# RWKV-7 stage of a hybrid trunk: one two-bank tile with one eviction, a block-diagonal solve, one state update for both heads, and the output products behind it

## The chip, the cores and the metric

The kernel runs on one core of a Trainium2 chip. The metric is the device time of one execution in microseconds (us). Engines are named as the profile names them: PE is the matrix engine (TensorE), PEld its weight loads, DVE the vector engine, ACT the scalar engine, POOL GpSimd, SP the engine that issues DMAs. PSUM is the memory that PE writes and DVE and ACT read; it has eight banks of 512 fp32 columns on 128 partitions.

## The reference

One layer of an encoder on `x` (1 x 4096 tokens x 1024 features): an RMS norm, one input projection whose columns feed three groups of heads, an output projection, an RMS norm and a residual. Group A is a Mamba-2 scan, group C a cross attention into 256 memory tokens. The change lies in group B, RWKV-7, with four heads of 64:

```python
def rwkv7_recurrence(r, w, k, v, a_vec, b_vec):
    """S_t = S_{t-1} (diag(w_t) + a_t^T b_t) + v_t^T k_t ; y_t = S_t r_t. Inputs (b,l,h,d) float32."""
    def step(S, inp):
        r_t, w_t, k_t, v_t, a_t, b_t = inp
        sa = jnp.einsum('bhij,bhj->bhi', S, a_t)
        S = S * w_t[:, :, None, :] + sa[..., None] * b_t[:, :, None, :] + v_t[..., None] * k_t[:, :, None, :]
        return S, jnp.einsum('bhij,bhj->bhi', S, r_t)
    ...

def rwkv7_group(u, mu, w0, w2, a0, a2, k_k, k_a, r_k, lnx_w, lnx_b):
    ...                                     # token shift, decay, k, kk, a from the projection u
    y = rwkv7_recurrence(rh, hs(decay), kh, vh, -kk, kk * ah)
    mean = jnp.mean(y, axis=-1, keepdims=True)
    var = jnp.mean(jnp.square(y - mean), axis=-1, keepdims=True)
    y = (y - mean) * lax.rsqrt(var + LNX_EPS)
    y = y * lnx_w... + lnx_b...
    bonus = jnp.sum(rh * kh * r_k, axis=-1, keepdims=True) * vh
    return ((y + bonus).reshape(b, l, W) * jax.nn.silu(g)).astype(u.dtype)
```

## The kernel before, in words

The program has three phases in one launch: `phase_a` (the Mamba-2 group, to about 750 us), `phase_b` (RWKV-7, to about 1640 us) and `phase_c` (attention and output projection). The code is written as generators; `weave` calls several of them in turn by weights, and the framework's scheduler, which has its own model of times, sets the order of every engine when the program is built. On the chip each engine then works through its row in that order and waits on semaphores where an operand isn't there.

`phase_b` goes over the 4096 tokens in 16 steps of `NT` = 256 tokens; a step has `NC_` = 4 chunks of `C` = 64 tokens, and the four heads are two pairs `p_` of two heads `h`. A pair fills the 128 partitions: head 0 lies in partitions 0 to 63 and head 1 in 64 to 127. What one step does is spread over three rounds of the loop: while step i is projected, the inverse of step i-1 is computed and the state runs through step i-2. The generators of a step:

- `stage1` projects the normalised tokens. Each weight goes through PE as three products of high and low parts (`w_hi`, `w_lo` by `hh`, `hl`; L137), 128x128 stationary and 256 columns. This is most of PE's work. It then forms r, k, v, the decay and so on.
- `gram2` makes, for each pair, four chunks and two heads, a 128x128 Gram product of `BK` by `AR` (L730). Head 0 goes to the PSUM bank `ps_yd`, head 1 to `ps_st`; DVE multiplies each bank by a mask into `AT` (L733).
- `solve2` inverts the triangular part of each 64x64 block: a recurrence on DVE for blocks of 16, then 32x16 products on PE (L785 to L815) that put larger blocks together in `TT`, two heads one above the other, 64 partitions by 64 columns each.
- `tokmaj` turns `v` and `BK` by transposes into rows of tokens (`UV`, `BKt`; L833, L846), and `stack` copies a part of `AR` under `AT` (L859).
- `stage3` is the serial part, chunk after chunk: ACT copies the state `ST` into `UV` (L871), POOL scales it to `S0` (L873), four products `AT` by `UV` give a right-hand side (L878), ACT copies that to `X` (L881), four 64x64 products `TT` by `X` solve (L885), DVE copies one head of the result to `UV` and ACT the other (L890), four products `BKt` by `UV` give the update (L895), and DVE adds it to `S0` for the next `ST` (L898). All of a chunk's products lie in one PSUM bank, `ps_yo`. After every second chunk, 16 output products of 64 columns follow: `rr` by `ST` (L912) and `AT` by `UV` (L915), into `ps_yd` for head 0 and `ps_st` for head 1.
- `stage4` normalises the outputs: DVE takes the means of both banks (L927), POOL scales them (L928), DVE centres both banks (L931); after that the banks are free. The result is scaled, gated and stored.

PSUM tiles come from one pool `ps` by tag: `tr` (2 buffers), `pj` (2), and `g`, `yo`, `yd`, `st` (one each). So `yd` and `st` serve the Gram products of step i-1 and the outputs of step i-2 by turns; the last step's Gram products go to `g` and `tr`.

Of the kernel before, what the change touches and what calls it, by code (L numbers as in the profile page):

```python
# [14 lines left out]
P = 128  # L15
# [12 lines left out]
def tile_hymba_trunk(  # L28
# [17 lines left out]

    def psum(tag, bufs):
        return ps.tile([P, 512], F32, name="ps_" + tag, tag=tag, bufs=bufs)
# [118 lines left out]
    def phase_a():  # L167
        a_l, a_r = ExitStack(), ExitStack()
# [324 lines left out]
    def phase_b(a_tail, a_l):  # L493
# [198 lines left out]
        left = lambda nm: b_l.enter_context(tc.tile_pool(name=nm, bufs=1, reuse_waits="tile"))  # L692
        bo.append(left("bo1"))
# [16 lines left out]
        nct = bi.tile([P, 16, 2 * NPC], F32, name="nct")  # L710
# [10 lines left out]

        def gram2(i, r):
            AR, BK, ec = r["AR"], r["BK"], r["ec"]
            AT = bi.tile([P, NPC, 2, P], F32, name="AT", tag="AT", bufs=2)
            for p_ in range(2):
                pas = (psum("g", 1), ps_tr()) if i == NS - 1 else (psum("yd", 1), psum("st", 1))
# [5 lines left out]
                for h, pa in enumerate(pas):  # L732
                    v.tensor_tensor(out=AT[:, p_ * NC_:(p_ + 1) * NC_, h, :], in0=pa.rearrange("p (x t) -> p x t", t=P),  # L733
                                    in1=amask.unsqueeze(1).broadcast_to([P, NC_, P]), op=ALU.mult)
                    yield
# [5 lines left out]
        def solve2(i, r):  # L741
            AT = r["AT"]
            for q in range(4):
# [31 lines left out]
            TT = bw.tile([P, NPC, 2, 32], F32, name="TT", tag="TT", bufs=2)  # L775
            Df = bi.tile([P, NPC, 32], F32, name="Df", tag="Df", bufs=2)
            Dt = bi.tile([P, NPC, 32], F32, name="Dt", tag="Dt")
# [74 lines left out]
        def stack(r):  # L852

            while "TT" not in r:
                yield
            AR, AT = r["AR"], r["AT"]
            for h in range(2):
                hs = slice(h * 64, h * 64 + 64)
                s.copy(out=AT[hs, :, h, 0:C].rearrange("p (b c) t -> p b c t", b=2), in_=AR[hs, :, :, 0, :])  # L859

        def stage3(i, r, nxt=None):
            AT, TT = r["AT"], r["TT"]
            pys = [psum("yd", 1), psum("st", 1)]
            sts = []
            for c_ in range(NC_):
# [16 lines left out]
                for p_, pc in enumerate(pcs):  # L882
                    for h in range(2):
                        hs = slice(h * 64, h * 64 + 64)
                        te.matmul(pch[hs, 128 + p_ * C:128 + p_ * C + C], lhsT=TT[hs, pc].rearrange("p a t -> p (a t)"),  # L885
                                  rhs=X[hs, p_, :], start=True, stop=True)
                yield
                for h in range(2):
                    hs = slice(h * 64, h * 64 + 64)
                    (s.copy if h else v.tensor_copy)(out=UV[hs, c_::NC_, h, :],  # L890
                                                     in_=pch[hs, 128:256].rearrange("p (b t) -> p b t", b=2))
# [402 lines left out]
```

## Time and profile before

| | |
|---|---|
| runs, us | 2230.16, 2230.88, 2237.77 (median 2230.88) |
| profiled execution | 2231.82 us, its span 2230.1 us |
| mean granted clock of PE | 0.983 of full speed |
| PE busy in 0 to 749 us (`phase_a`) | 717.96 of 749 us, DVE 594.15, ACT 395.01, POOL 274.65 |
| PE busy in 750 to 1640 us (`phase_b`) | 861.41 of 890 us, DVE 635.89, ACT 569.96, POOL 306.30 |
| PE busy in 1640 to 2230 us (`phase_c`) | 579.22 of 590.1 us, DVE 280.43, ACT 218.98, POOL 132.67 |

How to read the lines that follow: one execution was recorded by the hardware profiler. A line of the timeline gives the start of a group of like instructions in us, its length from first start to last end, the engine, the source line, the output and inputs by the program's names, the part of PE's array that the stationary operand uses, the shape, and behind x the number of records; in brackets stands how long the engine waited just before and for whom. A line of the groups gives the count, the busy time in us, the mean ns of one, and behind the bar the idle time of the engine just before them with what ended it. Lengths of matmuls overlap, since PE is pipelined; what a matmul costs PE is seen from start to start.

### The profile page before, as it was taken

Reading aid. Unit: us, or ns where it says so; the run is one execution under the profiler, and the core shown is the slowest. Engines: PE = TensorE matmul, PEld = TensorE weight load, DVE = VectorE, ACT = ScalarE, POOL = GpSimd, SP = SyncE. Lnnn points to the kernel's source line nnn. Section 1 sums busy time; section 2 is a strip of 40 time slices with the busy share of each in tenths; the row PEclk is TensorE's granted clock in tenths of the full one; section 3 lists DMA queues with packets and bytes.
Section 4 is the critical chain, followed back from the end, with each engine's and each line's share of the span. In section 5 each row is a group of like instructions: output and inputs, shape, how many; then the busy total and the mean of one; then the engine's idle time right before and its main releaser. Section 6 shows DMA issues by size and latency. Waiting matters only on the chain.

```text
span 2230.1 us, 51100 instructions
## 1 busy us (share of the span) xinstructions
PE 2159.6 (97%) x20705; PEld 1990.6 (89%) x20705; DVE 1511.5 (68%) x3442; ACT 1184.1 (53%) x2877; POOL 714.6 (32%) x1039
## 2 busy tenths in 40 slices
PE   5999999999999889999999999999899999999998
PEld 4999999999999888898899898898888888888986
DVE  5788878878888887577677777777574345454452
ACT  6555555545554565566666666677653334333341
POOL 1343434434343343343333433333112222222123
PEclk8999999999999999999999999999899999999999
DMA  6233222322233331112111112114243334334232
GB/s 204 86 135 103 96 96 93 141 91 96 96 114 132 114 99 39 44 44 76 50 49 44 44 48 78 49 59 146 91 161 132 130 112 143 127 120 137 103 123 76
DMA packets 83610, 218.86 MB, mean 98 GB/s; under 512 B 9191, under 2 KB 45486, under 8 KB 71086
## 3 DMA queue, kind: packets, MB, share of 16 engines
q1 hardware_dynamic: 82334, 215.59, 27.9%
q8 instruction: 163, 2.67, 0.5%
q14 instruction: 73, 0.60, 0.1%
q10 hardware_dynamic: 1040, 0.00, 0.0%
HBM read 152.00 MB, written 63.57 MB: 97 GB/s over the span
## 4 chain that ended last, share of the span: by engine, by line
PE 84%; DVE 6%; DMA 4%; ACT 3%; issue 1%; POOL 1%; SPq 0%; POOLq 0%; ACTq 0%; DVEq 0%
PE ps_pj L137 39%; PE ps_pj L147 8%; PE ps_yd L147 8%; PE ps_st L147 8%; DVE cc L296 2%; PE ps_yd L425 1%; PE ps_yo L878 1%; PE ps_pj L1143 1%; PE ps_yd L730 1%; PE ps_tr L126 1%; DMA w_st<-in_w_in_dram 1%; PE ps_tr L1131 1%; DMA R<-rowd 1%; PE ps_yo L885 1%; PE ps_st L417 1%
## 5 line engine op out<-in xcount | busy, mean ns | idle before, releaser
L137 PE MATMUL ps_pj<-hh,w_hi 128*128 128x256 f32 x2704 | 791.0, 293 | 6.8 <-ACT w_hi L78 4.0
L137 PE MATMUL ps_pj<-hh,w_lo 128*128 128x256 f32 x2704 | 781.1, 289 | 2.2 <-DVE w_lo L79 2.1
L137 PE MATMUL ps_pj<-hl,w_hi 128*128 128x256 f32 x2704 | 778.9, 288 | 0.0
L137 PEld LDWEIGHTS ps_pj<-hh,w_hi 128*128 128x128 f32 x2704 | 520.5, 192 | 17.9 <-ACT w_hi L78 4.6
L137 PEld LDWEIGHTS ps_pj<-hh,w_lo 128*128 128x128 f32 x2704 | 520.2, 192 | 9.7 <-DVE w_lo L79 3.5
L137 PEld LDWEIGHTS ps_pj<-hl,w_hi 128*128 128x128 f32 x2704 | 521.0, 193 | 7.1
L296 DVE SCALAR_TENSOR_TENSOR cc<-ux,cwh,cc 128x256 f32<-128x256 f32 x384 | 220.3, 616 | 16.0 <-ACT cc L293 12.2
L147 PE MATMUL ps_pj<-w_hi,hh 128*128 128x260 f32 (+1 forms) x528 | 156.6, 297 | 21.3 <-DVE dtr L270 15.8
L147 PE MATMUL ps_pj<-w_hi,hl 128*128 128x260 f32 (+1 forms) x528 | 153.0, 290 | 0.0
L147 PE MATMUL ps_pj<-w_lo,hh 128*128 128x260 f32 (+1 forms) x528 | 152.3, 289 | 0.0
L147 PEld LDWEIGHTS ps_pj<-w_hi,hh 128*128 128x128 f32 x528 | 102.5, 194 | 23.7 <-issue 16.0
L1150 DVE TENSOR_TENSOR ya<-ps_pj,ya 64x256 f32<-64x256 f32 x64 | 26.9, 421 | 121.6 <-ACT ya L1149 121.3
L1183 POOL TENSOR_TENSOR xr<-ot,xr 128x512 f32<-128x512 f32 x64 | 89.3, 1418 | 42.4 <-DVE ot L1182 42.4
L147 PEld LDWEIGHTS ps_pj<-w_lo,hh 128*128 128x128 f32 x528 | 102.5, 194 | 0.3
L147 PEld LDWEIGHTS ps_pj<-w_hi,hl 128*128 128x128 f32 x528 | 102.2, 194 | 0.0
L1177 POOL TENSOR_TENSOR sq<-sq 128x1 f32<-128x1 f32 x32 | 6.4, 201 | 292.7 <-ACT ot L1175 292.7
L147 PE MATMUL ps_yd<-wo0h,yh 128*128 128x512 f32 x248 | 98.3, 396 | 0.0
L147 PE MATMUL ps_st<-wo1l,yh 128*128 128x512 f32 x248 | 97.7, 394 | 0.4 <-DVE wo1l L1244 0.4
L147 PE MATMUL ps_st<-wo1h,yh 128*128 128x512 f32 x248 | 97.5, 393 | 0.0
L147 PE MATMUL ps_st<-wo1h,ylo 128*128 128x512 f32 x248 | 97.4, 393 | 0.0
L147 PE MATMUL ps_yd<-wo0h,ylo 128*128 128x512 f32 x248 | 97.3, 392 | 0.0
L147 PE MATMUL ps_yd<-wo0l,yh 128*128 128x512 f32 x248 | 97.2, 392 | 0.0
(474 smaller groups left out, 5102.1 us busy)
## 6 DMA issues: line engine op xcount, KB each, us to landing
hl<-hTd SPq DMA_DIRECT2D x32, 1024.0 KB
hh<-hTd SPq DMA_DIRECT2D x32, 1024.0 KB
xt<-in_x_dram SPq DMA_DIRECT2D x32, 512.0 KB
hTd<-hh SPq DMA_DIRECT2D x16, 1024.0 KB
hTd<-hl SPq DMA_DIRECT2D x16, 1024.0 KB
R<-rowd SPq DMA_DIRECT2D x32, 512.0 KB
xr<-in_x_dram SPq DMA_DIRECT2D x32, 512.0 KB
out_dram<-xr SPq DMA_DIRECT2D x32, 512.0 KB
```

What stands on the lines that cost most here:

```text
L126: te.transpose(pt[:, q * P:(q + 1) * P], src[:, k * P:(k + 1) * P], ident)
L137: te.matmul(outp, lhsT=a[:, k, :], rhs=b[:, k, :], start=(n == 0), stop=(n == 3 * KB - 1))
L147: te.matmul(outp, lhsT=a[:, k, tsl], rhs=b[:, k, 0:ncol], start=(n == 0), stop=(n == 3 * KB - 1))
L296: v.scalar_tensor_tensor(out=cc[:, b_, :], in0=ux[:, b_, j:j + NT], scalar=wj(j), in1=cc[:, b_, :], op0=ALU.mult, op1=ALU.add)
L417: te.matmul(pst[:, gr * 256:gr * 256 + 256], lhsT=q[c]["btm"][:, gr * P:(gr + 1) * P], rhs=q[c]["xde"][:, gr * 256:gr * 256 + 256], start= ...
L425: te.matmul(yd[hf * 64:hf * 64 + 64, h * 64:h * 64 + 64], lhsT=R[:, h, hf * 64:hf * 64 + 64], rhs=xdt[:, h * 64:h * 64 + 64], start=True, ...
L730: te.matmul(pa[:, c_ * P:(c_ + 1) * P], lhsT=BK[hs, p_, c_].rearrange("p a t -> p (a t)"), rhs=AR[hs, p_, c_].rearrange("p a t -> p (a t)" ...
L878: te.matmul(pch[hs, p_ * C:p_ * C + C], lhsT=AT[:, pc, h, 0:C], rhs=UV[:, pc, h, :], start=True, stop=True)
L885: te.matmul(pch[hs, 128 + p_ * C:128 + p_ * C + C], lhsT=TT[hs, pc].rearrange("p a t -> p (a t)"), rhs=X[hs, p_, :], start=True, stop=True)
L1131: te.transpose(pt[:, o:o + P], pr[:, t, m_ * P:(m_ + 1) * P], ident)
L1150: v.tensor_tensor(out=ya[hs], in0=pg[hs], in1=ya[hs], op=ALU.add)
L1183: g.tensor_tensor(out=xr[:, cs], in0=ots[n_], in1=xr[:, cs], op=ALU.add)
```

## The change

It has six parts.

1. The tags `yd` and `st` leave the pool `ps`. Each phase opens a pool of its own for them (`two_banks`); in `phase_b` that pool holds one tile `two` of two banks, [128, 2, 512], with one buffer.
2. `gram2` puts both heads in that tile, and one DVE instruction masks both banks (L751 of the changed kernel). `stage3` puts the outputs of both heads there, and `stage4` has one mean and one centring (L952, L955). The Gram products of the last step go to `g` and `tr` as before.
3. A tile `TTb` holds `TT` of both heads as a block-diagonal 128x128 matrix per chunk and pair. It is cleared once; `stack` fills the diagonal blocks with two POOL copies a step. The solve is then one 128x128 product over 64 columns per pair (L908), so two per chunk instead of four.
4. The update is one product per pair with all of `BKt` as stationary operand and both heads' `UV` as 128 columns (L917), two per chunk instead of four. Half of the result is not wanted; DVE adds the wanted parts to `S0` with two instructions on 64 partitions each (L922).
5. The output products stand under `tc.issue_after(upd.ins)`, which has them ordered right behind the last update product.
6. In `solve2` two pairs of work tiles share a buffer and `TT` has one buffer instead of two; a step waits with it until `stack` of the step before has run.

```diff
+        TTb = bw.tile([P, NPC, 2, C], F32, name="TTb")
+        g.memset(TTb, 0.0)
+        two = lambda: psx[-1].tile([P, 2, 512], F32, name="ps_two", tag="two", bufs=1)
 ...
-                pas = (psum("g", 1), ps_tr()) if i == NS - 1 else (psum("yd", 1), psum("st", 1))
+                big = None if i == NS - 1 else two()
+                pas = (psum("g", 1), ps_tr()) if big is None else (big[:, 0, :], big[:, 1, :])
 ...
-                for h, pa in enumerate(pas):
-                    v.tensor_tensor(out=AT[:, p_ * NC_:(p_ + 1) * NC_, h, :], in0=pa.rearrange("p (x t) -> p x t", t=P),
-                                    in1=amask.unsqueeze(1).broadcast_to([P, NC_, P]), op=ALU.mult)
+                    v.tensor_tensor(out=AT[:, p_ * NC_:(p_ + 1) * NC_].rearrange("p x h t -> p h x t"),
+                                    in0=big.rearrange("p h (x t) -> p h x t", t=P),
+                                    in1=amask.unsqueeze(1).unsqueeze(1).broadcast_to([P, 2, NC_, P]), op=ALU.mult)
 ...
-            TT = bw.tile([P, NPC, 2, 32], F32, name="TT", tag="TT", bufs=2)
+            while i > 0 and "stacked" not in rs_[i - 1]:
+                yield
+            TT = bw.tile([P, NPC, 2, 32], F32, name="TT", tag="TT")
 ...
+                g.tensor_copy(out=TTb[hs, :, h], in_=r["TT"][hs].rearrange("p c a t -> p c (a t)"))
                 s.copy(out=AT[hs, :, h, 0:C].rearrange("p (b c) t -> p b c t", b=2), in_=AR[hs, :, :, 0, :])
 ...
-            pys = [psum("yd", 1), psum("st", 1)]
+            py = two()
 ...
-                    for h in range(2):
-                        hs = slice(h * 64, h * 64 + 64)
-                        te.matmul(pch[hs, 128 + p_ * C:128 + p_ * C + C], lhsT=TT[hs, pc].rearrange("p a t -> p (a t)"),
-                                  rhs=X[hs, p_, :], start=True, stop=True)
+                    te.matmul(pch[:, 128 + p_ * C:128 + p_ * C + C], lhsT=TTb[:, pc].rearrange("p h t -> p (h t)"),
+                              rhs=X[:, p_, :], start=True, stop=True)
 ...
-                    for h in range(2):
-                        hs = slice(h * 64, h * 64 + 64)
-                        te.matmul(pch[hs, 256 + p_ * C:256 + p_ * C + C], lhsT=BKt[:, pc, hs], rhs=UV[:, pc, h, :],
-                                  start=True, stop=True)
+                    upd = te.matmul(pch[:, 256 + p_ * P:256 + p_ * P + P], lhsT=BKt[:, pc, :],
+                                    rhs=UV[:, pc].rearrange("p h t -> p (h t)"), start=True, stop=True)
 ...
-                v.tensor_tensor(out=STn, in0=S0, in1=pch[:, 256:384].rearrange("p (b t) -> p b t", b=2), op=ALU.add)
+                for h in range(2):
+                    hs = slice(h * 64, h * 64 + 64)
+                    v.tensor_tensor(out=STn[hs], in0=S0[hs], op=ALU.add,
+                                    in1=pch[hs, 256:512].rearrange("p (b h t) -> p b h t", b=2, h=2)[:, :, h, :])
 ...
+                    with tc.issue_after(upd.ins):
                         ...                               # the 16 output products of two chunks, as before
 ...
-            for h in range(2):
-                v.tensor_reduce(out=mean[:, h, :], in_=pys[h][:, 0:256].rearrange("p (c t) -> p c t", t=C), axis=AX.X, op=ALU.add)
+            v.tensor_reduce(out=mean, in_=pyv, axis=AX.X, op=ALU.add)
 ...
-            for h in range(2):
-                v.tensor_tensor(out=yc[:, h::2, :], in0=pys[h][:, 0:256].rearrange("p (c t) -> p c t", t=C),
-                                in1=mean[:, h, :].unsqueeze(2).broadcast_to([P, 4, C]), op=ALU.subtract)
+            v.tensor_tensor(out=yc.rearrange("p (c h) t -> p h c t", h=2), in0=pyv,
+                            in1=mean.unsqueeze(3).broadcast_to([P, 2, 4, C]), op=ALU.subtract)
```

The scheduler sets the order of all engines anew from this. Three places show how it moves instructions. A row of the built order gives the source line, the operation, output and inputs, the shape, and how many such instructions follow one another. Lines of the changed kernel have other numbers: L137 becomes L145, L878 L903, L885 L908, L895 L917, L912 and L915 become L938 and L941.

PE, around the output products of a regular step, before. `ps_pj` are projections, the numbers tell tiles of one name apart:

```order
L846 MATMUL ps_tr_17002<-ident_71,BK_15830 128x128 x4
L912 MATMUL ps_yd_16483<-ST_16856,rr_10881 64x64
L912 MATMUL ps_st_16484<-ST_16856,rr_10881 64x64
L912 MATMUL ps_yd_16483<-ST_16639,rr_10881 64x64
L912 MATMUL ps_yd_16483<-ST_16856,rr_10881 64x64
L912 MATMUL ps_st_16484<-ST_16639,rr_10881 64x64
L878 MATMUL ps_yo_16870<-UV_10879,AT_15768 64x64 x4
L912 MATMUL ps_st_16484<-ST_16856,rr_10881 64x64
L915 MATMUL ps_yd_16483<-UV_10879,AT_15768 64x64
L915 MATMUL ps_st_16484<-UV_10879,AT_15768 64x64
L137 MATMUL ps_pj_17017<-hh_15755,w_hi_10183 128x256
```

PE, the output products of a regular step in the changed kernel:

```order
L145 MATMUL ps_pj<-hh,w_hi 128x256
L917 MATMUL ps_yo<-UV,BKt 128x128 x2
L938 MATMUL ps_two<-ST,rr 64x64 x8
L941 MATMUL ps_two<-UV,AT 64x64 x8
L145 MATMUL ps_pj<-hl,w_hi 128x256
```

The output products stood in pieces, some between right-hand sides (L878) and projections; now all 16 stand in a row behind the update.

PE, around the solve and the update of a chunk, before; the 32x16 products belong to the inverse of another step:

```order
L137 MATMUL ps_pj<-hl,w_hi 128x256
L793 MATMUL ps_g<-Dt,pw 32x16 x12
L885 MATMUL ps_yo<-X,TT 64x64 x4
L793 MATMUL ps_g<-Dt,pw 32x16 x20
L137 MATMUL ps_pj<-hh,w_lo 128x256
```

The same work in the changed kernel, at a place where it stands closest:

```order
L642 MATMUL ps_tr<-sql,hones 128x256
L903 MATMUL ps_yo<-UV,AT 64x64
L145 MATMUL ps_pj<-hl,w_hi 128x256
L145 MATMUL ps_pj<-hh,w_lo 128x256
L903 MATMUL ps_yo<-UV,AT 64x64 x3
L856 MATMUL ps_tr<-ident,uv 128x128 x2
L869 MATMUL ps_tr<-ident,BK 128x128 x4
L908 MATMUL ps_yo<-X,TTb 128x64 x2
L917 MATMUL ps_yo<-UV,BKt 128x128 x2
L145 MATMUL ps_pj<-hh,w_hi 128x256
```

Between a solve and its update stood other work of PE; here the update follows the solve directly, and the six transposes that came elsewhere stand ahead of the solve.

DVE, from the means of the outputs to the mask eviction of the next Gram products, before:

```order
L927 TENSOR_REDUCE mean<-ps_yd 128x4
L927 TENSOR_REDUCE mean<-ps_st 128x4
L931 TENSOR_TENSOR yc<-ps_yd,mean 128x4x64
L931 TENSOR_TENSOR yc<-ps_st,mean 128x4x64
L679 TENSOR_TENSOR bv<-uv,ps_tr 128x512
L568 SCALAR_TENSOR_TENSOR ug<-ps_pj,pcol,tt 128x255
L936 TENSOR_REDUCE var<-yq 128x8
L568 SCALAR_TENSOR_TENSOR ug<-ps_pj,pcol,tt 128x255
L571 TENSOR_TENSOR cm<-ps_pj,pcol 128x2
L684 SCALAR_TENSOR_TENSOR ug<-tt,ug 128x512
L733 TENSOR_TENSOR AT<-ps_yd,amask 128x4x128
L733 TENSOR_TENSOR AT<-ps_st,amask 128x4x128
```

The same stretch in the changed kernel:

```order
L952 TENSOR_REDUCE mean<-ps_two 128x8
L818 TENSOR_TENSOR Dt<-Dt,ps_g 128x8x16
L576 SCALAR_TENSOR_TENSOR ug<-ps_pj,pcol,tt 128x255
L687 TENSOR_TENSOR bv<-uv,ps_tr 128x512
L822 STREAM_TRANSPOSE Df<-Dt 128x256
L823 TENSOR_SCALAR TT<-Dt,hm 128x8x32
L955 TENSOR_TENSOR yc<-ps_two,mean 128x2x4x64
L576 SCALAR_TENSOR_TENSOR ug<-ps_pj,pcol,tt 128x255
L579 TENSOR_TENSOR cm<-ps_pj,pcol 128x2
L960 TENSOR_REDUCE var<-yq 128x8
L751 TENSOR_TENSOR AT<-ps_two,amask 128x2x4x128
```

Means and centring followed one another; now other operations stand between them.

More of the change, by code (lines that the diff above doesn't have):

```diff
@@ L45, in tile_hymba_trunk, with two_banks @@
     dram = ctx.enter_context(tc.tile_pool(name="dram", bufs=1, space=bass.MemoryType.DRAM))
+    psx = []
+    def two_banks():
+        stack = ExitStack()
+        psx.append(stack.enter_context(tc.tile_pool(name=f"ps{len(psx)}", bufs=1, space=bass.MemoryType.PSUM)))
+        return stack
     def psum(tag, bufs):
-        return ps.tile([P, 512], F32, name="ps_" + tag, tag=tag, bufs=bufs)
+        return (psx[-1] if tag in ("yd", "st") else ps).tile([P, 512], F32, name="ps_" + tag, tag=tag, bufs=bufs)
     ps_tr = lambda: psum("tr", 2)
@@ L742, in solve2 @@
             AT = r["AT"]
+            nct = bi.tile([P, 16, 2 * NPC], F32, name="nct", tag="N")
             for q in range(4):
@@ L901, in stage3 @@
                 if c_ % 2 == 1:
[L902 to L916 removed]
+                    with tc.issue_after(upd.ins):
+                        for step in range(2):
+                            for p_ in range(2):
+                                for h in range(2):
+                                    hs = slice(h * 64, h * 64 + 64)
+                                    for par in range(2):
+                                        cq = c_ - 1 + par
+                                        pc = p_ * NC_ + cq
+                                        o = ((c_ // 2) * 2 + p_) * C
+                                        yo = py[par * 64:par * 64 + 64, h, o:o + C]
+                                        if step == 0:
+                                            te.matmul(yo, lhsT=rr[hs, p_, cq, :], rhs=sts[cq][hs, p_, :], start=(p_ == 0), stop=False,
+                                                      skip_group_check=True)
+                                        else:
+                                            te.matmul(yo, lhsT=AT[:, pc, h, C:2 * C], rhs=UV[:, pc, h, :], start=False, stop=True,
+                                                      skip_group_check=True)
                     if c_ == NC_ - 1:
[L918 removed]
+                        r["py"] = py
                     if nxt is not None:
@@ L1233, in phase_c @@
         late.close()
+        ctx.enter_context(two_banks())
         cw = ctx.enter_context(tc.tile_pool(name="cw", bufs=1, reuse_waits="tile"))
```

35 lines of the change are left out of this document (13 added, 22 removed).

## The prediction

> **What bounds the kernel now.** I read the page first: engine shares and the 40 slices.
>
> ```profile
> span 2230.1 us, 51100 instructions
> PE 2159.6 (97%) x20705; PEld 1990.6 (89%) x20705; DVE 1511.5 (68%) x3442; ACT 1184.1 (53%) x2877; POOL 714.6 (32%) x1039
> ...
> PE   5999999999999889999999999999899999999998
> ```
>
> TensorE is busy in nearly every slice. Since the ends of matmuls are modelled, busy alone proves no bound, so I next asked for the busy time of each engine in stretches of the RWKV stage (length, then PE, PEld, DVE, ACT, POOL, the granted clock, DMA), and for who waited for whom: in 1203.4 to 1440.1 us, five regular steps, PE waits for nobody.
>
> ```profile
> 1203.40:1440.10 236.70, 236.70 (x3161) 213.06 (x3160) 170.41 (x441) 154.46 (x380) 86.64 (x120) 1.00 0.14 52
> ...
> 1530.00:1660.00 130.00, 122.39 (x1208) 110.77 (x1206) 86.84 (x207) 79.60 (x201) 19.71 (x38) 0.91 0.39 133
> ```
>
> A regular step takes 236.7 / 5 = 47.3 us, with PE never idle and at full clock; DVE is busy 72%, ACT 65%, POOL 37%. So a step is as long as PE's row of starts, and another engine counts only where PE has to wait for it. The stage's tail (second row) leaves PE 7.6 us idle and costs it some clock. Ahead of the first Gram product and in the output phase PE's rows keep their order in the built program, so the change acts on the RWKV stage's 16 steps alone.
>
> **What one matmul costs PE.** The timeline of PE: start, length, and behind x the count of records. An fp32 matmul makes two records (passes).
>
> ```profile
> 1213.17 0.28 PE L137 MATMUL ps_pj<-hh,w_lo 128*128 128x256 f32 x1
> 1213.38 0.45 PE L885 MATMUL ps_yo<-X,TT 64*64 64x64 f32 x8
> 1213.76 0.39 PE L137 MATMUL ps_pj<-hh,w_hi 128*128 128x256 f32 x1
> 1213.98 0.28 PE L137 MATMUL ps_pj<-hl,w_hi 128*128 128x256 f32 x1
> ...
> 1215.15 0.28 PE L137 MATMUL ps_pj<-hh,w_hi 128*128 128x256 f32 x1
> 1215.27 0.60 PE L846 MATMUL ps_tr<-ident,BK 128*128 128x128 f32 x4
> 1215.62 0.36 PE L137 MATMUL ps_pj<-hl,w_hi 128*128 128x256 f32 x1
> 1215.83 0.28 PE L137 MATMUL ps_pj<-hh,w_lo 128*128 128x256 f32 x1
> ...
> 1216.18 0.28 PE L137 MATMUL ps_pj<-hh,w_lo 128*128 128x256 f32 x1
> 1216.30 0.28 PE L137 MATMUL ps_pj<-hh,w_hi 128*128 128x256 f32 x1
> 1216.51 0.45 PE L915 MATMUL ps_yd<-UV,AT 128*64 128x64 f32 x6
> 1216.89 0.38 PE L137 MATMUL ps_pj<-hl,w_hi 128*128 128x256 f32 x1
> 1217.11 0.27 PE L137 MATMUL ps_pj<-hh,w_lo 128*128 128x256 f32 x1
> ...
> 1217.55 0.45 PE L895 MATMUL ps_yo<-UV,BKt 128*64 128x64 f32 x8
> 1217.83 0.40 PE L915 MATMUL ps_st<-UV,AT 128*64 128x64 f32 x6
> ```
>
> Projections start 0.12 us apart (1216.18 to 1216.30). The eight passes of one solve product (L885), standing alone, stretch two such intervals from 0.24 to 0.81 us (1213.17 to 1213.98): they cost 0.57. Eight passes beside others of their form cost 0.28 (1217.55 to 1217.83), 0.035 each. An excursion of PE from the full array (128*128) to small tiles and back thus costs 0.57 - 0.28 = 0.29 besides its passes; by the six passes of L915 (1216.30 to 1217.11, again 0.57) it costs 0.57 - 0.21 = 0.36. I take 0.32, between the two. Four full-array passes (L846) stretch 0.24 to 0.68 (1215.15 to 1215.83): 0.11 each, with no excursion. A change between two small forms inside an excursion:
>
> ```profile
> 1209.51 0.22 PE L912 MATMUL ps_yd<-ST,rr 64*64 64x64 f32 x1
> 1209.66 0.45 PE L878 MATMUL ps_yo<-UV,AT 128*64 128x64 f32 x8
> 1210.04 0.32 PE L912 MATMUL ps_st<-ST,rr 64*64 64x64 f32 x2
> 1210.30 0.33 PE L915 MATMUL ps_yd<-UV,AT 128*64 128x64 f32 x2
> ```
>
> 0.79 from the first start to the last, for eleven passes worth 0.385: three changes at 0.13. The new full-array product over 64 columns is in no row; the nearest has the same 128x128 stationary operand and only 16 columns:
>
> ```profile
> 325.41 0.28 PE L137 MATMUL ps_pj<-hh,w_hi 128*128 128x256 f32 x1
> 325.53 0.29 PE L329 MATMUL ps_g<-dta,triu 128*128 128x16 f32 x2
> 325.67 0.36 PE L137 MATMUL ps_pj<-hl,w_hi 128*128 128x256 f32 x1
> 325.87 0.28 PE L137 MATMUL ps_pj<-hh,w_lo 128*128 128x256 f32 x1
> ```
>
> 0.46 - 0.24 = 0.22 for two passes, again 0.11. Since 16 and 128 columns cost the same, I take 0.11 for the 64 columns of the solve and the 128 of the update; the bounds are 0.11 above and a small tile's 0.035 below.
>
> [...]
>
> **The change, part by part.** Counts are for the whole stage, from the two built orders.
> - Excursions: 283 before, 199 after. The block-diagonal solve and the merged update no longer leave the full array, and the output products come 16 in a row behind the update instead of in pieces: -84 x 0.32 = -26.9 us.
> - Changes of form inside excursions: 200 before, 103 after: -97 x 0.13 = -12.6.
> - Small passes removed: 512 of L885 and 512 of L895, -1024 x 0.035 = -35.8.
> - Full passes added: 256 and 256, 512 x 0.11 = +56.3.
> - So PE's row gets 19.0 us shorter, about 1.2 a step, and nothing covers it in the regular steps.
> - Thin cover. The new order spreads work less evenly between dependent products. At seven places the update stands right behind the solve product whose copy it needs; before, the thinnest such place has 0.4 us of PE work between them. Of the other places between dependent products of a chunk, 14 have under 1 us of cover, 10 before. Two stretches of the timeline before price it:
>
> ```profile
> 918.68 0.69 PE L885 MATMUL ps_yo<-X,TT 64*64 64x64 f32 x8 [0.41 <-ACT X L881]
> 919.77 0.28 DVE L890 COPY UV<-ps_yo 64x128 f32<-64x128 f32 x1
> 920.08 0.26 ACT L890 COPY UV<-ps_yo 64x128 f32<-64x128 f32 x1
> 920.39 0.37 PE L895 MATMUL ps_yo<-UV,BKt 128*64 128x64 f32 x1
> ...
> 1511.92 0.45 PE L885 MATMUL ps_yo<-X,TT 64*64 64x64 f32 x8 [0.20 <-ACT X L881]
> 1513.35 0.45 PE L895 MATMUL ps_yo<-UV,BKt 128*64 128x64 f32 x8 [0.43 <-ACT UV L890]
> ```
>
> From solve to update it is 1.43 to 1.71 us. The new solve fills 0.44 of that, so PE idles 1.0 to 1.3 at each of the seven; I take 1.0, regular steps having the emptier queues: +7.0. The four further places at up to 0.43 (the brackets) are under +1.7; I put +0.5, as most lack only 0.1 to 0.2. Behind the waiting update on PE stand the next projections, which can't pass it; they wait with it.
> - DVE and POOL, groups of the same five steps (busy, mean ns, then idle before):
>
> ```profile
> L733 DVE TENSOR_TENSOR AT<-ps_yd,amask 128x512 f32<-128x512 f32 x10 | 6.9, 688 | 5.6 <-PE ps_yd L730 5.6
> L898 DVE TENSOR_TENSOR ST<-S,ps_yo 128x128 f32<-128x128 f32 x20 | 5.8, 288 | 10.2 <-PE ps_yo L895 7.9 <-ACT UV L837 2.1
> L931 DVE TENSOR_TENSOR yc<-ps_yd,mean 128x256 f32<-128x256 f32 x5 | 2.1, 425 | 1.8 <-POOL mean L928 1.8
> L647 POOL TENSOR_TENSOR BK<-uk,lw 64x512 f32<-64x512 f32 x10 | 13.5, 1352 | 0.4
> ```
>
> 256 columns take 0.425 and 512 take 0.688, so 0.263 per 256 more: a two-bank Gram eviction takes 1.21 instead of 2 x 0.69, twice a step -0.33; mean and centring -0.16 each. The state sum becomes two of 64 partitions, 0.29 each at most: +1.15 a step. DVE +0.5 in 47.3, hidden by its idle 28%; without that cover it is +8 us for the stage. The two copies a step to the block-diagonal tile cost POOL at most 1.35 each (L647 reads two inputs of 512 columns) and at least nothing, against 63% idle; between the last product of the inverse and the first solve stand about 6 us of PE work, and ACT's copies and these need under 3.5. Zero, as are the one memset and the shared buffers of the inverse, whose steps are serial already.
>
> Sum: -19.0 + 7.5 = -11.5 us. The profiled execution took 2231.8 us, so 2220.3 for its like; the median of the runs lies 0.9 below it: **2219.4 us**.
>
> **Rivals.**
> 1. Thin cover eats it. For: 30 places have under 1.5 us of cover where 13 had; 0.4 at each of the 23 besides the seven is +9. Against: many lie where ACT's and DVE's queues are short. 2226 to 2231.
> 2. Slower: the two-bank tile is one buffer. Gram products of head 0 could start once their own bank was read; now all wait until both banks are centred, and in the built DVE order five other operations stand between mean and centring.
>
> ```profile
> 1240.34 0.41 DVE L931 TENSOR_TENSOR yc<-ps_st,mean 128x256 f32<-128x256 f32 x1
> 1243.66 0.71 PE L730 MATMUL ps_yd<-AR,BK 64*128 64x128 f32 x4
> ```
>
> Now 2.9 us lie between them. If PE comes to wait 0.7 us a step here, the gain is gone; from 1.4 on it is slower by 0.5%; the five operations at some 0.45 each would be 2.2, +36: 2250.
> 3. The full passes over 64 columns are cheaper, 0.06 and not 0.11: 256 x 0.05 = -13, 2206. Against: L329.
> 4. Slower by the tiles given up: where groups stood in company, four small tiles cost 0.28 and the full form 0.44, +0.16 x 128 groups = +20.5. It turns the sum of PE's row where an excursion is worth under 0.1. Against: 0.29 and 0.36. 2240 to 2250. [...]
>
> **How the numbers follow.** A run of this kernel tells about 0.5% (11 us) from no change. The forecast (thin cover 2 to 13, excursions 0.29 to 0.36: 2211 to 2227) has 0.58, of which 0.33 is faster by more than that and 0.25 not. Rival 1 has 0.18, rival 2 0.08, rival 3 0.10, rival 4 0.03, and 0.03 goes to slower by something unnamed. Faster 0.33 + 0.10 = 0.43; within 0.25 + 0.18 = 0.43; slower 0.14. The range drops rivals 2 and 4, the unnamed and half of rival 3: 2206 to 2236.
>
> **What would show it.** Right: solve and update records in the 128*128 form 0.11 apart and fewer excursions; regular steps of unequal length that average 46 to 46.8 us; waits of the update for the solve's copies near 1.0 us, once in two steps. Wrong: waits of Gram products for the centring (rival 2), many short waits of PE for X and UV (rival 1), solve starts 0.06 apart (rival 3). A granted clock below 1.00 in the regular steps would upset every term.

## The result, and the profile after

The changed kernel takes 2255.1 us (median of 4 runs, 2252.4 to 2260.61), the kernel before 2231.0 us on the same chip: ratio 1.011, 95% interval 1.0089 to 1.0131. It is 24 us slower, where 2219.4 us, a gain of 11.5 us, was forecast. The page of the changed kernel begins:

```profile
span 2250.7 us, 50122 instructions
...
PE 2144.4 (95%) x20193; PEld 1992.1 (89%) x20193; DVE 1537.8 (68%) x3444; ACT 1183.6 (53%) x2877; POOL 740.6 (33%) x1072
```

PE's busy time went down from 2159.6 to 2144.4 us, and yet the span is 20.6 us longer: PE's idle time, span less busy time, rose from 70.5 to 106.3 us. The stretches of the RWKV stage (length, PE, PEld, DVE, ACT, POOL, granted clock) show where; first six regular steps and the tail of the kernel before, then the same work of the changed kernel:

```profile
1156.10:1440.10 284.00, 284.00 (x3793) 255.66 (x3792) 204.46 (x528) 185.34 (x456) 103.96 (x144) 1.00 0.14 52
1440.10:1634.70 194.60, 185.36 (x2240) 167.33 (x2240) 132.79 (x342) 124.90 (x311) 50.28 (x76) 0.94 0.26 87
```

```profile
1160.50:1448.90 288.40, 276.23 (x3634) 255.79 (x3635) 213.54 (x529) 185.01 (x457) 119.22 (x159) 0.99 0.14 51
1448.90:1653.90 205.00, 185.76 (x2099) 169.80 (x2098) 141.61 (x347) 127.20 (x313) 54.67 (x82) 0.93 0.27 92
```

In six regular steps PE's busy time got 7.8 us shorter (284.0 to 276.2), but 12.2 us of idle time came in where there was none. In the tail PE is busy as long as before, and idle for 10 us more. What PE waited for in the stage, lines picked from the list (total in us, times, the longest); before, then changed:

```profile
PE ps_yo L895 <- ACT UV L890: 3.1, 4, 2.0
...
PE ps_yo L885 <- ACT X L881: 1.0, 3, 0.4
```

```profile
PE ps_yo L917 <- ACT UV L913: 14.3, 13, 3.4
PE ps_pj L145 <- DVE cm L579: 5.2, 8, 1.9
PE ps_yo L908 <- ACT X L906: 4.0, 4, 1.1
PE ps_tr L970 <- DVE yc L963: 2.9, 3, 1.4
PE ps_tr L856 <- ACT t L974: 2.9, 3, 1.0
...
PE ps_tr L869 <- DVE sq L643: 2.4, 3, 0.8
```

The update waits for the solve's copy 13 times. The rest are waits that the kernel before hardly had: projections (L145) for a PSUM bank that DVE has not read yet (L579), transposes (L856, L869) for a bank `ps_tr` that ACT (L974) or DVE (L643) has not read yet, and transposes (L970) for their operand `yc`. The longest wait, in the timeline:

```profile
915.40 0.56 PE L908 MATMUL ps_yo<-X,TTb 128*128 128x64 f32 x4
...
916.07 0.28 DVE L913 COPY UV<-ps_yo 64x128 f32<-64x128 f32 x1
916.52 2.48 ACT L767 COPY nct<-AT 32x256 f32<-32x256 f32 x4
...
919.02 0.26 ACT L913 COPY UV<-ps_yo 64x128 f32<-64x128 f32 x1
...
919.34 0.78 PE L917 MATMUL ps_yo<-UV,BKt 128*128 128x128 f32 x3 [3.38 <-ACT UV L913]
```

DVE's half of the copy ran at once; ACT's half stood behind four copies of the inverse (2.48 us) in ACT's row. The update follows the solve directly on PE, so PE had nothing else for 3.38 us. In the regular steps the same happens on a smaller scale, once in two steps:

```profile
1329.05 0.56 PE L908 MATMUL ps_yo<-X,TTb 128*128 128x64 f32 x4
...
1329.71 0.28 DVE L913 COPY UV<-ps_yo 64x128 f32<-64x128 f32 x1
...
1330.20 0.45 ACT L575 ACTIVATE tt<-ps_pj,omu 128x256 f32<-128x256 f32 x1
...
1330.68 0.26 ACT L913 COPY UV<-ps_yo 64x128 f32<-64x128 f32 x1
...
1330.99 0.71 PE L917 MATMUL ps_yo<-UV,BKt 128*128 128x128 f32 x4 [1.39 <-ACT UV L913]
```

Here ACT works on the projections' results first (L575), and PE waits 1.39 us. Three stretches of 3.4 us from 916.2 us on (the seventh figure is the granted clock):

```profile
916.20:919.60 3.40, 0.26 (x2) 0.27 (x3) 0.72 (x2) 3.03 (x6) 1.43 (x2) 1.00 0.00 0
919.60:923.00 3.40, 3.31 (x44) 2.65 (x43) 3.30 (x10) 1.37 (x4) 0.50 (x2) 0.50 0.20 77
923.00:926.40 3.40, 2.81 (x24) 2.78 (x24) 3.11 (x16) 2.03 (x6) 0.29 (x2) 1.00 0.02 5
```

After the idle stretch PE runs the next 3.4 us at half clock (0.50), counted as busy (3.31 of 3.40 us). Over the whole execution, the time lost to a lower clock (the length of each clock record times one minus its granted clock, summed) rose from 37.9 to 48.7 us. So the change of the span splits into three parts: work as at full clock (busy less clock loss) 2121.7 before and 2095.7 after, -26.0; clock loss +10.8; idle +35.8. The split is rough: where PE idles inside a slow stretch it takes too much from the work. Of these differences 3.3 us of work and 1.7 of clock loss lie ahead of 740 us, where the change does not act; between 740 us and 530 us before the end they are -22.1, +8.5 and +34.1.

### The profile page after: what moved, and what is told of

Read it like the earlier page. It is cut to its first block, busy times and chain, and to the rows that moved or that the text cites. A ratio compares the mean times of both kernels' runs of the same rounds, so it can differ in the third digit from the quotient of the medians.

```text
span 2250.7 us, 50122 instructions
## 1 busy us (share of the span) xinstructions
PE 2144.4 (95%) x20193; PEld 1992.1 (89%) x20193; DVE 1537.8 (68%) x3444; ACT 1183.6 (53%) x2877; POOL 740.6 (33%) x1072
## 4 chain that ended last, share of the span: by engine, by line
PE 74%; DVE 11%; ACT 7%; DMA 3%; issue 2%; POOL 2%; SPq 0%; POOLq 0%; DVEq 0%; ACTq 0%
PE ps_pj L145 33%; PE ps_pj L155 8%; PE ps_yd L155 8%; PE ps_st L155 8%; DVE cc L304 1%; PE ps_yd L433 1%; PE ps_pj L1167 1%; PE ps_two L744 1%; PE ps_yo L917 1%; PE ps_tr L134 1%; ACT nct L767 1%; PE ps_tr L1155 1%; ACT w_hi L86 1%; DVE T L787 1%; PE ps_st L425 1%
## 5 line engine op out<-in xcount | busy, mean ns | idle before, releaser
L145 PE MATMUL ps_pj<-hh,w_hi 128*128 128x256 f32 x2704 | 790.3, 292 | 12.4 <-DVE cm L579 5.2
L145 PE MATMUL ps_pj<-hh,w_lo 128*128 128x256 f32 x2704 | 779.0, 288 | 2.2 <-DVE w_lo L87 2.1
L145 PE MATMUL ps_pj<-hl,w_hi 128*128 128x256 f32 x2704 | 778.5, 288 | 0.0
L145 PEld LDWEIGHTS ps_pj<-hh,w_hi 128*128 128x128 f32 x2704 | 522.5, 193 | 22.8 <-ACT w_hi L86 5.2
L145 PEld LDWEIGHTS ps_pj<-hh,w_lo 128*128 128x128 f32 x2704 | 522.1, 193 | 6.9 <-DVE w_lo L87 3.5
L145 PEld LDWEIGHTS ps_pj<-hl,w_hi 128*128 128x128 f32 x2704 | 522.5, 193 | 5.7
L304 DVE SCALAR_TENSOR_TENSOR cc<-ux,cwh,cc 128x256 f32<-128x256 f32 x384 | 220.1, 615 | 15.0 <-ACT cc L301 11.2
L155 PE MATMUL ps_pj<-w_hi,hh 128*128 128x260 f32 (+1 forms) x528 | 155.7, 295 | 22.5 <-DVE dtr L278 17.6
L155 PE MATMUL ps_pj<-w_hi,hl 128*128 128x260 f32 (+1 forms) x528 | 151.8, 288 | 0.0
L155 PE MATMUL ps_pj<-w_lo,hh 128*128 128x260 f32 (+1 forms) x528 | 151.1, 286 | 0.2 <-DVE w_lo L87 0.2
L155 PEld LDWEIGHTS ps_pj<-w_hi,hh 128*128 128x128 f32 x528 | 101.4, 192 | 25.1 <-issue 17.8
L155 PEld LDWEIGHTS ps_pj<-w_lo,hh 128*128 128x128 f32 x528 | 101.4, 192 | 0.4 <-DVE w_lo L87 0.4
L155 PE MATMUL ps_yd<-wo0h,yh 128*128 128x512 f32 x248 | 98.5, 397 | 2.8 <-DVE yc L955 2.3
L155 PEld LDWEIGHTS ps_pj<-w_hi,hl 128*128 128x128 f32 x528 | 101.0, 191 | 0.0
L155 PE MATMUL ps_st<-wo1h,yh 128*128 128x512 f32 x248 | 97.6, 394 | 1.6 <-ACT wo1h L1268 1.6
L155 PE MATMUL ps_st<-wo1l,yh 128*128 128x512 f32 x248 | 97.6, 393 | 0.0
L155 PE MATMUL ps_st<-wo1h,ylo 128*128 128x512 f32 x248 | 97.4, 393 | 0.0
L155 PE MATMUL ps_yd<-wo0h,ylo 128*128 128x512 f32 x248 | 97.3, 392 | 0.0
L155 PE MATMUL ps_yd<-wo0l,yh 128*128 128x512 f32 x248 | 97.2, 392 | 0.0
```

The source lines that it names most:

```text
L145: te.matmul(outp, lhsT=a[:, k, :], rhs=b[:, k, :], start=(n == 0), stop=(n == 3 * KB - 1))
L155: te.matmul(outp, lhsT=a[:, k, tsl], rhs=b[:, k, 0:ncol], start=(n == 0), stop=(n == 3 * KB - 1))
L304: v.scalar_tensor_tensor(out=cc[:, b_, :], in0=ux[:, b_, j:j + NT], scalar=wj(j), in1=cc[:, b_, :], op0=ALU.mult, op1=ALU.add)
```

## Experiments

Theory *cover*: PE's row did get shorter, and the order that was built anew leaves PE idle between dependent products. Rival *price*: the full-array products cost more than 0.11 us a pass. Rival *group*: one part, the two-bank tile or the grouped output products, does the harm. Theories *copies*, *product*, *wait*, *order* and *content* came up on the way and are explained where they are used. Each time is a median, set against the kernel before on the same chip (2230.2 to 2231.1); work, clock loss and idle are differences from the trace of before, in us.

| run | us | ratio, interval | work | clock loss | idle |
|---|---|---|---|---|---|
| changed kernel | 2255.1 | 1.0110, 1.0089 to 1.0131 | -26.0 | +10.8 | +35.8 |
| e1 solve | 2259.5 | 1.0132, 1.0117 to 1.0148 | -5.2 | +10.6 | +23.1 |
| e2 update | 2237.8 | 1.0032, 1.0021 to 1.0043 | +18.5 | -9.0 | -3.3 |
| e3 two banks | 2223.9 | 0.9975, 0.9963 to 0.9986 | -11.2 | -10.9 | +13.4 |
| e4 outputs behind update | 2208.6 | 0.9907, 0.9891 to 0.9922 | -23.4 | -2.9 | +7.2 |
| e5 solve, ACT copies | 2241.3 | 1.0050, 1.0034 to 1.0065 | +6.1 | -4.1 | +6.2 |
| e6 solve, small products | 2250.6 | 1.0091, 1.0077 to 1.0106 | +3.5 | -3.9 | +18.6 |
| e7 two banks, outputs behind | 2220.7 | 0.9953, 0.9936 to 0.9971 | -32.9 | +0.9 | +16.8 |
| e8 changed, other copies | 2248.3 | 1.0073, 1.0056 to 1.0090 | -27.3 | +6.6 | +29.7 |
| e9 before, weight 26 | 2204.1 | 0.9880, 0.9867 to 0.9894 | -21.0 | -11.4 | +2.3 |
| e10 before, weight 22 | 2235.2 | 1.0021, 1.0012 to 1.0030 | -1.0 | -5.3 | +9.8 |
| e11 solve, weight 16 | 2234.1 | 1.0015, 1.0006 to 1.0024 | -6.7 | -0.2 | +11.9 |
| e12 changed, weight 34 | 2275.0 | 1.0207, 1.0192 to 1.0223 | -35.2 | +30.9 | +44.1 |
| e13 changed, weight 20 | 2252.8 | 1.0105, 1.0086 to 1.0125 | -34.5 | +23.7 | +36.4 |
| e14 changed, outputs free | 2263.5 | 1.0153, 1.0131 to 1.0174 | +1.6 | +10.7 | +21.2 |
| e15 outputs behind, other weights | 2203.7 | 0.9881, 0.9861 to 0.9901 | -33.4 | -3.7 | +10.1 |

The last three columns are of one profiled execution each, which can lie some us beside the median (7.4 us for e8), and carry the roughness of the split.

**Each part alone.** e1 puts parts 3 and 6 of the change into the kernel before:

```diff
+                g.tensor_copy(out=TTb[hs, :, h], in_=r["TT"][hs].rearrange("p c a t -> p c (a t)"))
 ...
-                        te.matmul(pch[hs, 128 + p_ * C:128 + p_ * C + C], lhsT=TT[hs, pc]..., rhs=X[hs, p_, :], ...)
+                    te.matmul(pch[:, 128 + p_ * C:128 + p_ * C + C], lhsT=TTb[:, pc]..., rhs=X[:, p_, :], ...)
```

> The kernel before with the block-diagonal solve alone (the tile TTb, the two POOL copies a step, the shared buffers and the wait that make room for it). Priced start to start by the trace of before, PE's row of the built order gets 3.9 us shorter (31 excursions and 33 inner changes fewer, 512 small passes out, 256 full ones in). Theory cover (the time after is lost where the new order leaves PE idle between dependent products): eight places between solve and update have under 1 us of PE work where before had four, and the solve's wait for X has less too, so PE's idle time grows by 5 to 15 us: 2232 to 2245. Theory price (the full-array products cost more than 0.11 us a pass, idle time is an effect of little weight): idle within 4 us of before, busy up by 5 to 10: 2236 to 2241. Theory group (the loss comes from the two-bank tile or the grouped output products alone): no loss here, 2224 to 2231.

e2 has the merged update and its two additions (L917, L922) alone:

```diff
-                        te.matmul(pch[hs, 256 + p_ * C:256 + p_ * C + C], lhsT=BKt[:, pc, hs], rhs=UV[:, pc, h, :], ...)
+                    te.matmul(pch[:, 256 + p_ * P:256 + p_ * P + P], lhsT=BKt[:, pc, :], rhs=UV[:, pc]..., ...)
```

> The kernel before with the merged state update alone (two 128x128 products of 128 columns per chunk, two additions of 64 partitions). Priced as above, PE's row gets 8.4 us longer (256 full passes for 512 small ones, excursions 288 against 283 since the order is made anew). Theory cover: one place between solve and update has under 1 us of cover where before had four, so idle time is as before or 1 to 3 us less: 2234 to 2240. Theory price: a full pass dearer than 0.11 adds 5 to 10 more: 2242 to 2250. Theory group: 2228 to 2240.

e3 has the two-bank tile with its evictions, mean and centring alone:

```diff
-            pys = [psum("yd", 1), psum("st", 1)]
+            py = two()
```

> The kernel before with the two-bank tile alone (one mask eviction, one mean, one centring for both heads; Gram products and outputs in it). Priced as above, PE's row gets 9.1 us shorter. Theory cover: six places between solve and update under 1 us against four, eleven against four under 1.5 us between right-hand side and solve: idle time up by 3 to 9 us: 2225 to 2231. Theory price: nothing dear is in it: 2220 to 2223. Theory group, with the single two-bank buffer as the cause: waits of Gram products for the centring of 0.7 us a step or more, 2232 to 2245.

e4 has one line more than the kernel before (and the name `upd` that it needs):

```diff
+                    with tc.issue_after(upd.ins):
                         ...                               # the 16 output products
```

> The kernel before with the output products ordered right behind the last update product of the second chunk, and nothing else. Priced as above, PE's row gets 15.0 us shorter, since output products stand 16 in a row. Theory cover: between right-hand side and solve seven places under 1 us against four, between solve and update ten under 1.5 us against five: idle time up by 5 to 10 us: 2220 to 2227. Theory price: 2214 to 2219. Theory group, with the row of 16 products as the cause (dependent products behind it are pushed back, and what stood between them is gone): idle time up by 15 us or more, 2231 to 2240.

e1 lost 29 us, more than any theory gave it; its work hardly changed (-5.2, and -3.9 priced), and idle time and clock loss together took 33.7. e2 lost 7.5, in the ranges of *cover* and *group* and under *price*'s; but its work rose by 18.5 and not by the 8.4 priced, and the time came out lower because 9.0 us of clock loss went away, which no theory had. So e2's time alone decides nothing here. e3 gained 6.3, between the ranges of *cover* and *price*, with 13.4 us more idle time where *cover* had 3 to 9; *group* falls for the tile. e4 gained 21.6, more than any theory gave it: its idle time rose as *cover* had it, by 7.2, but its work fell by 23.4 and not by 15.0. *Group* falls altogether. Where the output products run, PE shows all 32 passes in a row:

```profile
1213.66 0.45 PE L895 MATMUL ps_yo<-UV,BKt 128*64 128x64 f32 x8 [0.42 <-ACT UV L890]
1214.05 0.27 PE L913 MATMUL ps_yd<-ST,rr 64*64 64x64 f32 x2
...
1214.84 0.29 PE L916 MATMUL ps_st<-UV,AT 128*64 128x64 f32 x4
```

About 0.8 us from the first start to the last. Summed start to start over six regular steps, the output products cost 3.67 us a step before (0.057 a pass) and 2.01 in e4 and in the changed kernel. The price of a full-array pass itself can be read in e2, where the update stands between two projections:

```profile
1211.58 0.28 PE L137 MATMUL ps_pj<-hl,w_hi 128*128 128x256 f32 x1
1211.69 0.61 PE L893 MATMUL ps_yo<-UV,BKt 128*128 128x128 f32 x4
1212.06 0.36 PE L137 MATMUL ps_pj<-hh,w_lo 128*128 128x256 f32 x1
1212.26 0.28 PE L137 MATMUL ps_pj<-hh,w_hi 128*128 128x256 f32 x1
```

1211.58 to 1212.26 less two projections at 0.12 leaves 0.44 for four passes: 0.11 each, as forecast, so *price* falls for the pass. But in e2's regular steps only one update in four stands like this. The other three stand beside small products and take 0.54 to 0.64 us from their start to the next product's, where this one takes 0.37: the change of form comes on top, and the update costs 2.19 us a step against 1.28 before. The four small products had taken 0.23 to 0.38 us at these places before, so where they stood in company the merging makes PE's row longer.

**What is dear in the solve.** e5 is e1 with the two copies on ACT, e6 is e1 with small products:

```diff
-                g.tensor_copy(out=TTb[hs, :, h], in_=r["TT"][hs]...)
+                s.copy(out=TTb[hs, :, h], in_=r["TT"][hs]...)                      # e5
 ...
-                    te.matmul(pch[:, 128 + ...], lhsT=TTb[:, pc]..., rhs=X[:, p_, :], ...)
+                        te.matmul(pch[hs, 128 + ...], lhsT=TTb[hs, pc, h], rhs=X[hs, p_, :], ...)   # e6, for each head
```

> The solve alone as in e1 (2259.5 us, 29 us over before), with the two copies into the block-diagonal tile on ACT instead of POOL. In e1's trace the POOL copies of a step end at 1263.0 us and the first solve stands at 1266.6, behind four transposes of the stage after; before, it stood 2.6 us behind the copy of X. Theory copies (the step from TT to the first solve is what costs: the copies queue on POOL behind other work, and the order built around them puts the solve late): with ACT's copies, which stand beside the others of that step, 2232 to 2242. Theory product (the full-array solve itself is dear: 2.07 us a step in e1 against 1.54 before, and it pushes PE into half-clock stretches): no change, 2253 to 2262. Theory wait (the shared buffers and the wait for the stacked flag): 2253 to 2262 too.

> e1 with everything of the solve part (tile, POOL copies, shared buffers, wait), but the products themselves four small ones of 64x64 as before, read from the diagonal blocks. Theory copies: most of the 29 us stays, 2248 to 2260. Theory product: 2230 to 2238. Theory wait: 2250 to 2262; from theory copies it is told by e5.

Both came out as theory *copies* had it (e6 is also in the range of *wait*, which e5 speaks against): 18 of e1's 29 us go with the POOL copies, and 20 stay without the full-array product. e8 tried the same in the changed kernel (one copy on DVE, one on ACT):

```diff
-                g.tensor_copy(out=TTb[hs, :, h], in_=r["TT"][hs]...)
+                (s.copy if h else v.tensor_copy)(out=TTb[hs, :, h], in_=r["TT"][hs]...)
```

> The changed kernel with the copy of head 0 into the block-diagonal tile on DVE and that of head 1 on ACT, instead of both on POOL; nothing else. Theory copies: the 20 us or so that e1 loses by them come back, 2230 to 2242. Theory product or wait: 2250 to 2258.

Only 7 us came back, which no theory gave: 2248.3 is above *copies*' range and just below that of the others. And the copies are as short as ever in e11:

```profile
L864 POOL COPY TTb<-TT x32: 602/614/970, 858.9 to 1588.5; 64x512 f32<-64x512 f32 x32
```

(minimum, median and maximum in ns). e11 is e1 with one weight of the interleaving changed, not one instruction, POOL copies included:

```diff
-                weave((chain(gram2(i - 1, ...), solve2(i - 1, ...)), 14), (chain(*back, stack(r1)), 26), (first, 30),
+                weave((chain(gram2(i - 1, ...), solve2(i - 1, ...)), 16), (chain(*back, stack(r1)), 26), (first, 30),
```

> e1 (the block-diagonal solve with the POOL copies, 2259.5 us) with the weight of the inverse's part 16 instead of 14, instructions the same as in e1. Theory copies (POOL copies cost some 18 us by themselves): 2252 to 2264. Theory order (e1 got an unlucky order, and part of its 29 us is not the solve's): 2238 to 2250.

2234.1 us, 25 under e1 and under even the range of *order*. So theory *copies* falls too, and *product* and *wait* with it: moving the copies had made the order of all engines anew, and most of what was dear in e1 was its order.

**The same instructions in another order.** e9 changes the weight 30 to 26 in the kernel before, e10 the weight 26 to 22:

```diff
+                weave((..., 14), (chain(*back, stack(r1)), 26), (first, 26),      # e9
+                weave((..., 14), (chain(*back, stack(r1)), 22), (first, 30),      # e10
```

> The kernel before with one number changed: the weight by which the projections are interleaved is 26 instead of 30. Not one instruction differs, only the order that is built. PE's row has 236 excursions instead of 283 and is 13.6 us shorter by the prices of the trace of before. Theory content (each part of the change costs what its instructions cost, and a rebuilt order is worth little by itself): within 0.5%, 2220 to 2242. Theory order (the order that comes out, excursions and cover, is worth 10 us or more either way whatever made it anew): 2212 to 2220.

> The kernel before with another number changed: the weight of the chunk-by-chunk part is 22 instead of 26, all instructions the same. PE's row is 5.1 us shorter by the same prices, thin places as many as before, but the regular steps of the built order are of unlike content and no longer all the same. Theory content: 2224 to 2236. Theory order: cover is lost where a long step follows a short one, 2236 to 2250.

e9 gained 27 us, more than any part of the change and more than theory *order* gave it. Its regular steps take 45.3 us, and PE still never waits:

```profile
1146.20:1417.90 271.70, 271.70 (x3795) 249.53 (x3793) 196.67 (x528) 187.04 (x456) 106.05 (x144) 1.00 0.15 54
```

e10 lost 4 us, still in the range of *content*, with 9.8 us more idle time and less clock loss. *Content* is refuted by e9 and by e11. e12 gives the changed kernel weight 34 for the projections, and with it 17 thin places between solve and update instead of 8; e13 gives it weight 20 for the inverse, with fewer:

```diff
+                weave((..., 14), (chain(*back, stack(r1)), 26), (first, 34),      # e12
+                weave((..., 20), (chain(*back, stack(r1)), 26), (first, 30),      # e13
```

> The changed kernel with the projections' weight 34 instead of 30, instructions the same. PE's row is 2 us shorter by the prices of before, but 17 places between solve and update have under 1 us of PE work where the changed kernel has eight. Theory cover (a thin place costs about 1 us of waiting, and more where it slows PE's clock): 9 more places, 2262 to 2275. Theory price (waits are an effect of little weight): 2250 to 2257.

> The changed kernel with the weight of the inverse's part 20 instead of 14, instructions the same. The built order has two places between solve and update under 0.5 us of PE work where the changed kernel has seven, one place of that kind between right-hand side and solve instead of three, and PE's row is 4.2 us shorter by the prices of before. Theory order (most of the changed kernel's loss is the cover its order lacks): 2225 to 2240. Theory content (its solve, update and POOL copies cost that much in any order): 2247 to 2258.

e12 is 20 us above the changed kernel with the same instructions and less work, in the range of *cover*. But the waits are not those that *cover* had counted; the first three of e12:

```profile
PE ps_yo L917 <- ACT UV L913: 13.9, 14, 3.6
PE ps_tr L856 <- ACT UV L860: 10.0, 8, 1.5
PE ps_pj L145 <- DVE cm L579: 7.1, 5, 1.9
```

With nine more thin places the update waits as often and as long as in the changed kernel (14.3 us, 13 times). What is new are waits of transposes for a bank that ACT has not read (L860), 8.3 us more idle time in all, and 20.1 us more clock loss. So e12 shows that the order alone is worth 20 us, by idle time and clock; that the time fell into *cover*'s range by the places counted is not shown, and was luck. e13 came out where *content* had it, and its waits tell why:

```profile
PE ps_yo L903 <- ACT UV L896: 21.8, 11, 3.4
PE ps_pj L145 <- DVE cm L579: 6.7, 4, 3.8
PE ps_yo L917 <- ACT UV L913: 3.1, 5, 1.0
```

The wait of the update fell from 14.3 to 3.1 us, and a wait of the right-hand sides for ACT's copy of the state took its place, 11 times and 2.0 us each. Two of a chunk's three links had got more cover, and the third had lost it; clock loss rose as well, by 12.9 us against the changed kernel. Theory *order* missed here, since it had counted the first two links only.

**Parts together.** e7 is the two-bank tile and the ordered output products on the small products of before; e14 is the changed kernel without the line of e4; e15 is e4 with weights 16 and 26 for 14 and 30:

```diff
-                    with tc.issue_after(upd.ins):                                  # e14, against the changed kernel
+                weave((..., 16), (chain(*back, stack(r1)), 26), (first, 26),      # e15, against e4
```

> The changed kernel without its solve and update parts: the two-bank tile and the output products ordered behind the update, on the small products of before. If the parts add (-6.3 in e3, -21.6 in e4): 2202 to 2206. If shortening PE's row twice uses up the cover (the built order has 12 places between right-hand side and solve under 1 us of PE work, e4's 7, before 4): 2208 to 2220. Against the changed kernel's 2255 it tells what solve and update cost together: 29 + 7.5 = 37 if they add, so 2218.

> The changed kernel without the ordering of the output products behind the update; everything else as changed. By the prices of before PE's row is 20.8 us longer, with 58 more excursions and 44 more inner changes; places under 0.5 us between solve and update are four instead of seven. If the ordering saves in the changed kernel what it saved alone (21.6 us in e4): 2270 to 2282. If it mostly takes away cover there: 2240 to 2255.

> e4 (the kernel before with the output products ordered behind the update, 2208.6 us) with the weights 16 for the inverse and 26 for the projections instead of 14 and 30. PE's row is 2.8 us shorter than e4's and 4.2 us shorter than e9's; 14 places between right-hand side and solve under 1 us, e4 seven, e9 four. If e4's gain is the part's own (16 output products in a row, 1.66 us a step): it stays under 2212 in this order too, 2198 to 2210. If it was the order's luck: 2212 to 2235.

The parts do not add: e3 and e4 together would be -28, e7 is -10, just above its upper range, with 9.6 us more idle time and 3.8 more clock loss than e4 for 9.5 less work. The changed kernel lies 34 us above e7, near the 37 that e1 and e2 lost; after e11 that agreement proves little. e14 came out between its two ranges: the line of e4 is worth 8 us in the changed kernel, not 21.6. It saves 27.6 us of work there and gives 14.6 back as idle time (the profiled runs). e15 stayed under 2212 and, at 2203.7, is level with e9 (2204.1). The gains of e4 and e9 did not add here, though e15 differs from e9 in the weight of the inverse too. Both times are 1.2% below the kernel before and 2.3% below the changed one.

## Why the prediction was wrong, step by step

- *Excursions, passes and form changes* (-19.0): right in the total, and the output products show the mechanism (3.67 us a step to 2.01); what each kind of product would gain or lose was not forecast. The -26.0 of the split is too large; counted start to start in the RWKV stage, with products in half-clock stretches scaled by 0.120 / 0.213 (see the last section), PE's work fell by 20.5 us: the output products by 24.7, projections by 12.9 and Gram products by 10.0 (by fewer changes of form beside them, it seems, which was not tested), while the update rose by 12.5 and solve, right-hand sides, transposes and inverse by 14.6 together. The merged update loses by itself, as e2 showed; the terms had that too (512 passes at 0.035 out, 256 at 0.11 in).
- *Thin cover* (+7.5): the step that failed. Idle time rose by 35.8 us, and clock loss, which had no term, by 10.8. The seven places without cover came as counted, but they cost 11.0 us, 1.6 each and not 1.0: the reason for 1.0, that queues are emptier in regular steps, did not hold, since ACT's half of the copy stood behind other work, as in the two timelines above (1.39 us at 1331 us, 3.38 at 919 us). Six places with some cover waited too, 3.4 us in all. With the solve's and the right-hand sides' waits the chain of a chunk took 20.1 us, against 4.7 before, so 15.4 more. The other 20 us or so are mostly waits outside this chain, of transposes and projections, largely for banks that ACT or DVE still had to read; they were not counted at all. And a wait was priced by its own length, while the clock halved behind some of them (0.50 for 3.4 us behind the 3.38 us at 919 us); a clock below 1.00 in the regular steps was named as a thing that would upset every term, and it came (0.99 over the six steps).
- *DVE and POOL at nothing*: the sizes were right. The two-bank eviction took 1.22 us against the estimate of 1.21, a state addition 0.28, a copy 0.62 (median) between bounds of 0 and 1.35, and PE waits for no copy on POOL. The cover was not: projections wait 5.2 us for DVE (L579), and whether its added work or its new order makes it late was not separated.
- *Rival 2, Gram products waiting for the centring*: did not happen. Its price was 0.7 us a step and more (its last sum is off: 2219.4 and 36 make 2255, not 2250, so that the measured time agrees with it by chance); PE waited once in the whole stage ahead of a two-bank Gram product, 0.7 us, for the mask eviction, and once for the centring, 2.3 us, with the first output projection of the next phase (L155); e3 with this tile is faster than before.
- *Rival 1, thin cover eats the gain*: the right direction with 0.18, at 2226 to 2231. Its mechanism, waits in the chain of a chunk, is under half of the idle time that came; the rest is named above.
- *Rival 3, cheap full passes*, did not come: a solve between two projections takes 0.44 for four passes, 0.11 each, in the changed kernel. *Rival 4, tiles given up*, is wrong for the whole, as the work got shorter; for the update alone, in company, its mechanism is what e2 shows.
- What would show it: steps of unequal length came, and waits of the update once in two steps, but the steps' mean was 48.1 us and not 46 to 46.8, and the waits were 1.39 and not near 1.0.

What is shown is where the time went: less work, and more idle time and clock loss than it saved. That the order is to blame is shown for e1 (e11) and by the size of what one weight does (e9, e12). Open is how much of the 24 us belongs to the changed kernel itself. With three orders each it took 2253 to 2275, the kernel before 2204 to 2235; the best of the one is above the worst of the other, but three orders are no proof that none is better.

## What to carry to other kernels

Where a scheduler orders the whole program, an edit has two effects, its instructions and the new order of everything else, and the second can be the larger: one weight, with no instruction changed, was worth -27 us here, while the parts of the change, each in its own new order, were worth -22 to +29. Run a control that changes the order alone before you credit or blame a part, and tune the order again for the version that you keep. When you count cover, follow every link of the serial chain, and every PSUM bank that must be read before it is written again (transposes waited 10.0 us for such a bank in e12), through the rows of all engines, and price a wait with what the clock takes behind it (here 3.4 us at 0.50 behind one of 3.38 us).

## What the runs showed of the hardware

In the traces of before and the changed kernel the clock loss comes in 11 and 15 stretches at a granted clock of 0.50. They last 3.41 us or multiples of it, but for the last of each, which lasts to the end of the execution, and within a run they start on one fixed grid of 3.41 us. Sorted by PE's idle time in the grid's window just before (windows at full clock, 820 to 1650 us, the profiles of before, the changed kernel and e1 to e8): of 2127 windows with under 0.5 us of idle time 1 was followed by half clock, of 87 with 0.5 to 1.0 us 7, of 51 with 1.0 to 1.5 us 16, and of 43 with 1.5 us or more 40. So 1.5 us or more of idle time in one window, as two waits of some 0.8 us make it, mostly brought a stretch at half clock here (40 of 43). What that costs shows in the changed kernel, at the end of one (1264.4 to 1267.8 us):

```profile
1266.70 0.41 PE L145 MATMUL ps_pj<-hh,w_lo 128*128 128x256 f32 x1
1266.91 0.41 PE L145 MATMUL ps_pj<-hh,w_hi 128*128 128x256 f32 x1
...
1267.90 0.29 PE L145 MATMUL ps_pj<-hh,w_lo 128*128 128x256 f32 x1
1268.02 0.28 PE L145 MATMUL ps_pj<-hh,w_hi 128*128 128x256 f32 x1
```

Projections start 0.213 us apart in half-clock stretches and 0.120 outside (medians of the stage), so 3.41 us of them hold 1.9 us of work: an estimated 1.5 us is lost, a little less than the half of the split above.
